# Layer kernel on one Trainium2 core: low parts and sums of squares from POOL to DVE in three stages, and nine gated blocks loaded early

## The chip, the core and the metric

The kernel runs on one core of a Trainium2 chip. The metric is the device time of one execution in microseconds (us), as the median of several runs. A separate profiled execution of the same kernel gives the trace. The engines are PE (TensorE matmul; PEld is its weight load), DVE (VectorE), ACT (ScalarE), POOL (GpSimd) and SP (SyncE), whose queue issues the transfers.

## The reference, cut to what matters

One layer acts on two groups of tokens: 256 prompt tokens and 1024 latent tokens, both of width 1024, with the same weights. The hidden width of the two feed-forward nets (ffn1 and ffn2) is 2816.

```python
def rms_norm(x, g):
    y = xf * lax.rsqrt(jnp.mean(xf * xf, axis=-1, keepdims=True) + EPS)
    return (y * g.astype(jnp.float32)).astype(x.dtype)

def swiglu(h, w_in, w_out):
    gate, up = jnp.split(h @ w_in, 2, axis=-1)
    return (jax.nn.silu(gate) * up) @ w_out

def layer(x, cond, p, lb, lam_init, ctx_cache=None, rope=None):
    ...
    h = rms_norm(x, p['norm_ffn1']) * (1.0 + sc1) + sh1
    x = x + 0.5 * g1 * swiglu(h, p['w_ffn1_in'], p['w_ffn1_out'])
    h = rms_norm(x, p['norm_mix']) * (1.0 + sc2) + sh2
    mix, k_ctx, v_ctx, s_ctx = token_mix(h, p, lb, lam_init, ctx_cache, rope)
    x = x + g2 * mix
    h = rms_norm(x, p['norm_ffn2']) * (1.0 + sc3) + sh3
    x = x + 0.5 * g3 * swiglu(h, p['w_ffn2_in'], p['w_ffn2_out'])
    return x, k_ctx, v_ctx, s_ctx
```

The token mixing between the two nets is not touched by the change, save for the sums of squares of its norm.

## The kernel before, in words

**Arithmetic.** A float32 product is made from split operands. ACT rounds a block to its high part (a CAST), another engine subtracts this from the block and gets the low part (a TENSOR_TENSOR, TT), and PE multiplies high by high, high by low and low by high. So each block of weights or of activations costs one cast, one subtraction and three matmuls for each output tile.

**Stages.** Each net has four: prompt in, latents in, latents out, prompt out. In the trace, ffn1's run at 34.6 to 190.5 us, to about 650, to 885.4 and to 961.5; mixing with attention lies between; ffn2's run at 1936.2 to 2072.4, to about 2499, to 2732.2 and to the end.

- Prompt in (`wload`, L99): 44 units of weights, 128x1024, named `ffn1g0` to `ffn1g21` (gate) and `ffn1u0` to `ffn1u21` (up); a trailing `r` is the raw load, `h` the high and `l` the low part. `wh` and `wl` have four buffers each, so the parts of a unit are made a few units ahead of PE. In this stage (`half` set) DVE and POOL take the low parts in turn. In ffn1, DVE also forms the sums of latents (`o0a`, `o0b`, `x0b` and the like) for the stage that follows.
- Latents out (`latents_out`, `out_blocks`): seven products of a Strassen-like scheme in the order 1, 2, 5, 6, 7, 3, 4, each over eleven blocks p. For each block PE does 12 matmuls of 128x512 with the weight block `ffn1w_{p}b` and the block of gated values `ffn1w_{p}g`. Names carry p and not the product, so each name comes seven times. ACT casts both; POOL makes the low part of b, DVE that of g (L758). For products 5, 6, 7 and 3 DVE also forms the sum that is the block b (`ffn1s`, `ffn1qhh`, `ffn1qhl`), and drains the finished products from PSUM into the latents (`xr0a` and others: SCALAR_TENSOR_TENSOR, STT). With the block tiles in four buffers, the parts are made up to three blocks ahead.
- Gated values go by way of `g_d` in device memory: the last steps of latents in write `g_d` from `ffn1g10c` to `ffn1g10x` and `ffn1t`. Five blocks of product 1 are loaded into a resident tile (`self.g1`, in the trace `ffn1qhl<-g_d`); every later one goes through the four-buffer tag `gr` (`ffn1w_5gr<-g_d`), asked for two blocks ahead.
- Prompt out (`prompt_out_blocks`): 22 steps, each with two weight blocks `ffn1pw` (128x512; the first low part on DVE, the second on POOL) and one block of values `ffn1pvv` (128x256, on DVE), for 24 matmuls of 128x256.
- Sums of squares (`sumsq`, L345): ACT squares (`sq`), and POOL (first half) or DVE (second half) adds to `sacc`, as the drained latents come out; a norm follows (its `pm` matmul waits for `sacc`).

**Order.** A scheduler sets the order of the instructions on each engine from the order of the code and the tiles that come free; once built, each engine works through its list strictly in order. SP issues its loads and stores in order too, and a transfer that waits for its tile or for its data holds those behind it. All instructions are recorded under L49, where a helper class passes them on, so they are told apart by the names of their tiles.

Of the kernel before, what the change touches and what calls it, by code (L numbers as in the profile page):

```python
# [9 lines left out]
F32 = mybir.dt.float32  # L10
# [3 lines left out]
ALU = mybir.AluOpType  # L14
# [4 lines left out]
P = 128  # L19
# [46 lines left out]
class Kern:  # L66
# [9 lines left out]
    def pool(self, name, space=None, side=None):  # L76
        kw = {} if space is None else {"space": space}
        if space != DRAM:
            kw["reuse_waits"] = "tile"
        if side is not None:  # L80
            kw["side"] = side
        return self.tc.tile_pool(name=name, bufs=1, **kw)
# [16 lines left out]
    def wload(self):  # L99
        nc = self.nc  # L100
        if not self.rawq:
            self.rload()
        raw, name = self.rawq.popleft()
        shape = list(raw.shape)
        hi = self.wp.tile(shape, F32R, tag="wh", bufs=4, name=name + "h")
        nc.scalar.copy(hi, raw)
        lo = self.wp.tile(shape, F32R, tag="wl", bufs=4, name=name + "l")
        self.nw += 1
        eng = nc.vector if self.half and self.nw % 2 else nc.gpsimd
        eng.tensor_tensor(lo, raw, hi.bitcast(F32), op=ALU.subtract)  # L110
        self.wready.append((hi, lo))
        while len(self.rawq) < self.nraw and self.wq:
            self.rload()
# [231 lines left out]
    def sumsq(self, tp, c, d):  # L345
        nc = self.nc
        n = CH[c][1]
        h = d // 4
        acc = self.acc[c]
        if h not in acc:  # L350
            acc[h] = tp.tile([P, n], F32, tag="t", bufs=self.tb, name=f"sacc{c}_{h}")
            nc.scalar.activation(acc[h], self.x[c][d], AF.Square)
        else:
            sq = tp.tile([P, n], F32, tag="t", bufs=self.tb, name=f"sq{c}_{d}")
            nc.scalar.activation(sq, self.x[c][d], AF.Square)
            (nc.vector if h else nc.gpsimd).tensor_tensor(acc[h], acc[h], sq, op=ALU.add)
        self.nsq[c] += 1
        if self.nsq[c] == KD:
            self.nsq[c] = 0
            return True  # L360
# [308 lines left out]

    def out_resident(self, hp, wout, name):  # L670

        t = [hp.tile([P, m, 512], F32, tag=g, name=f"{name}q{g}")
             for m, g in ((8, "hh0"), (8, "hl0"), (4, "hh2"), (2, "hl2"), (8, "hl1"))]
        fl = [x[:, j] for x, m in zip(t, (8, 8, 4, 2)) for j in range(m)]
        self.a11, self.a12 = fl[:NPR], fl[NPR:]
        self.s3, self.g1 = [t[4][:, j] for j in range(3)], [t[4][:, j] for j in range(3, 8)]
        for p in range(8):
            self.out_w(wout, self.a11[p], p, 0, 0)
            if p < 5:
                self.nc.sync.dma_start(self.g1[p], self.g_d[:, 0, p])  # L680

    def out_w(self, wout, t, p, i, j):
        self.nc.sync.dma_start(t, wout[0, (2 * p + j) * P:(2 * p + j + 1) * P, i * 512:(i + 1) * 512])
# [11 lines left out]
    def out_blocks(self, wout, name, hp, xp, pool):  # L695

        nc = self.nc
        V, G = nc.vector, nc.gpsimd
        keys = [(i, p) for i in self.OUT for p in range(NPR)]
        raws = {}  # L700
        xs = deque(self.x_pieces(xp))

        def load(j):
            if j >= len(keys):
                return
            i, p = keys[j]
            n_ = f"{name}w{i}_{p}"
            if j < 5:
                g = self.g1[j]
            else:  # L710
                g = pool().tile([P, 512], F32, tag="gr", bufs=4, name=n_ + "gr")
                nc.sync.dma_start(g, self.g_d[:, i - 1, p])
            a = None
            if i == 1:
                if p >= 8:
                    self.out_w(wout, self.a11[p], p, 0, 0)
            elif i == 2:
                self.out_w(wout, self.a12[p], p, 0, 1)
            elif i in (5, 7, 4):
                a = self.raw(pool, [P, 2, 512], n_ + "r")  # L720
                if i in (5, 7):
                    self.out_w(wout, a[:, 0], p, 1, 0)
                if i in (5, 4):
                    self.out_w(wout, a[:, 1], p, 1, 1)
            if xs and j >= 2 and j % 2 == 0:
                nc.sync.dma_start(*xs.popleft())
            if i == 5 and p == 4:
                self.x_move(pool(), 2, True)
            raws[j] = g, a
        s_ = None  # L730
        load(0)
        load(1)
        for j, (i, p) in enumerate(keys):
            load(j + 2)
            g, a = raws.pop(j)
            n_ = f"{name}w{i}_{p}"
            if i == 5 and p == 0:
                s_ = hp.tile([P, 8, 512], F32, tag="hh1", name=f"{name}s")
                s_ = [s_[:, q] for q in range(8)] + self.s3
            if i == 1:  # L740
                a = self.a11[p]
            elif i == 2:
                a = self.a12[p]
            elif i == 5:
                V.tensor_tensor(s_[p], a[:, 0], a[:, 1], op=ALU.add)
                a = s_[p]
            elif i == 6:
                V.tensor_tensor(s_[p], s_[p], self.a11[p], op=ALU.subtract)
                a = s_[p]
            elif i == 7:  # L750
                V.tensor_tensor(self.a11[p], self.a11[p], a[:, 0], op=ALU.subtract)
                a = self.a11[p]
            elif i == 3:
                V.tensor_tensor(self.a12[p], self.a12[p], s_[p], op=ALU.subtract)
                a = self.a12[p]
            else:
                a = a[:, 1]
            yield self.block(a, n_ + "b", G), self.block(g, n_ + "g", V)  # L758

    def latents_out(self, name, pop, g, ng, done, then):  # L760
        nc = self.nc
# [36 lines left out]
    def prompt_out_blocks(self, wout, name, pool):  # L798
        nc = self.nc
        raws = {}  # L800

        def load(f):
            if f < NF:
                r = self.raw(pool, [P, D], f"{name}pw{f}")
                nc.sync.dma_start(r, wout[0, f * P:(f + 1) * P, :])
                v = pool().tile([P, NP], F32, tag="gr", bufs=4, name=f"{name}pv{f}")
                nc.sync.dma_start(v, self.gp_d[:, f])
                raws[f] = r, v
        load(0)
        load(1)  # L810
        for f in range(NF):
            load(f + 2)
            r, v = raws.pop(f)
            w = [self.block(r[:, h * 512:(h + 1) * 512], f"{name}pw{f}{h}", nc.gpsimd if h else nc.vector)
                 for h in range(2)]
            vv = pool().tile([P, 2, NP], F32R, tag="gv", bufs=3, name=f"{name}pvv{f}")
            self.split(vv[:, 0], vv[:, 1], v)
            yield w, vv
# [957 lines left out]
```

## Time and profile before

| | |
|---|---|
| median of 3 runs | 2801.65 us (2801.49 to 2803.29) |
| profiled execution | 2805.98 us |
| its span in the trace | 2803.9 us |
| mean granted PE clock | 0.983 |
| DMA | 429.29 MB, mean 153 GB/s |

The profiled execution is 2.08 us longer than its span and 4.33 us longer than the median. In the views below, a row of the timeline reads: start, duration, engine, line, operation, tile written <- tiles read, shapes, count, and in brackets the idle time before with what ended it. Durations overlap where an engine is pipelined, so the pitch of back-to-back instructions is less than the duration of one. A row of the waits gives the engine and its tile, what it waited for, the total in us, the number of times and the longest.

### The profile page before, as it was taken

How to read it: one execution, taken by the hardware profiler on the slowest of the kernel's cores; microseconds unless marked ns; L12 is line 12 of the kernel's file. 1: busy time of each engine (PE TensorE's matmuls, PEld its weight loads, DVE VectorE, ACT ScalarE, POOL GpSimd, SP SyncE). 2: the span in 40 equal slices, each digit the busy share in tenths (PEclk: the TensorE clock that was granted, in tenths of full speed). 3: DMA queues.
4: the chain of work that ended last, by engine and by line, in shares of the span. 5: the costliest groups of instructions: out<-in, count | busy, mean ns of one | idle time of the engine just before them, and what ended most of it. 6: DMA issues, size and time to landing. Idle time of an engine off the chain costs nothing.

```text
span 2803.9 us, 43921 instructions
## 1 busy us (share of the span) xinstructions
PE 2685.2 (96%) x17070; PEld 2344.7 (84%) x17070; DVE 1675.1 (60%) x2158; ACT 1116.9 (40%) x1896; POOL 1274.7 (45%) x902
## 2 busy tenths in 40 slices
PE   7999999999899999999999899999999999999999
PEld 6887777887688889898989888888988888877789
DVE  3955554655877636465555488747745555558754
ACT  4642222323345423232323477745432333324344
POOL 2454444443545636455554122165454444435443
PEclk8999999999999999999999999999999999999999
DMA  9765656338635531323224944385643233357455
GB/s 304 232 185 184 194 181 196 103 98 271 199 119 191 189 103 55 102 71 96 76 68 124 213 104 115 132 276 160 189 137 113 94 97 110 104 192 249 132 180 185
DMA packets 412245, 429.29 MB, mean 153 GB/s; under 512 B 20621, under 2 KB 314757, under 8 KB 409989
## 3 DMA queue, kind: packets, MB, share of 16 engines
q1 hardware_dynamic: 411856, 426.43, 49.1%
q8 instruction: 134, 2.20, 0.3%
q14 instruction: 75, 0.61, 0.1%
q10 hardware_dynamic: 180, 0.06, 0.0%
HBM read 326.79 MB, written 99.61 MB: 152 GB/s over the span
## 4 chain that ended last, share of the span: by engine, by line
PE 76%; DVE 10%; DMA 4%; issue 4%; POOL 3%; ACT 2%; SPq 1%; ACTq 0%; DVEq 0%; POOLq 0%
PE ffn2po L49 6%; PE ffn1po L49 5%; PE mob L49 4%; PE ffn2pp L49 2%; PE ffn2pu L49 2%; PE ffn2pg L49 2%; PE ffn1pu L49 1%; PE ak0b L49 1%; PE aq0b L49 1%; PE ak1b L49 1%; PE ffn1pg L49 1%; SPq L49 1%; PE ffn1pp L49 1%; PE ada L49 1%; PE hg1b L49 1%
## 5 line engine op out<-in xcount | busy, mean ns | idle before, releaser
L49 PE MATMUL ffn1pp<-ffn1pvv,ffn1pw 128*128 128x256 f32 x528 | 67.9, 290 | 3.7 <-DVE ffn1pvv L49 3.3
L49 PEld LDWEIGHTS ffn1pp<-ffn1pvv,ffn1pw 128*128 128x128 f32 x528 | 66.2, 197 | 5.2 <-DVE ffn1pvv L49 4.1
L49 PE MATMUL ffn2pp<-ffn2pvv,ffn2pw 128*128 128x256 f32 x528 | 64.0, 283 | 0.0
L49 PEld LDWEIGHTS ffn2pp<-ffn2pvv,ffn2pw 128*128 128x128 f32 x528 | 63.6, 192 | 0.1
L49 POOL TENSOR_TENSOR ffn2pw<-ffn2pw,ffn2pw 128x512 fp32r<-128x512 f32 x22 | 28.9, 1316 | 35.8 <-ACT ffn2pw L49 34.2
L49 POOL TENSOR_TENSOR hl<-nt,hh 128x256 fp32r<-128x256 f32 (+1 forms) x20 | 22.4, 1121 | 40.1 <-ACT hh L49 37.7
L49 POOL TENSOR_TENSOR ffn1pw<-ffn1pw,ffn1pw 128x512 fp32r<-128x512 f32 x22 | 33.2, 1512 | 13.2 <-ACT ffn1pw L49 13.1
L49 ACT ACTIVATE nt<-nt,mt,sv 128x256 f32<-128x256 f32 (+1 forms) x40 | 25.7, 680 | 29.9 <-DVE sv L49 17.7
L49 DVE TENSOR_TENSOR sacc<-sacc,sq 128x512 f32<-128x512 f32 (+1 forms) x18 | 29.3, 1630 | 12.3 <-ACT sq L49 12.0
L49 ACT CAST ffn2pw<-ffn2pw 128x512 fp32r<-128x512 f32 x44 | 26.9, 620 | 15.5 <-PE ffn2pp L49 8.8
L49 DVE TENSOR_TENSOR ffn2pw<-ffn2pw,ffn2pw 128x512 fp32r<-128x512 f32 x22 | 17.0, 772 | 25.8 <-ACT ffn2pw L49 25.8
L49 ACT CAST ffn1pw<-ffn1pw 128x512 fp32r<-128x512 f32 x44 | 26.1, 615 | 12.6 <-DMA ffn1pw<-w_ffn_out 6.4
L49 PE MATMUL ada<-wada,cst 128*32 128x256 f32 x448 | 30.0, 385 | 0.0
L49 PE MATMUL ffn1po<-ffn1w_5g,ffn1w_5b 128*128 128x512 f32 x84 | 22.8, 422 | 6.0 <-ACT ffn1w_5g L49 5.3
L49 DVE TENSOR_REDUCE a_0mx<-a_0S 128x1 f32<-128x1536 f32 x8 | 14.1, 1758 | 24.0 <-PE a_0S L49 23.9
L49 PE MATMUL ffn2po<-ffn2w_5g,ffn2w_5b 128*128 128x512 f32 x84 | 22.9, 426 | 5.5 <-ACT ffn2w_5g L49 5.5
L49 PE MATMUL ffn1po<-ffn1w_4g,ffn1w_4b 128*128 128x512 f32 x84 | 22.6, 420 | 4.4 <-POOL ffn1w_4b L49 4.4
L49 PEld LDWEIGHTS ffn1po<-ffn1w_5g,ffn1w_5b 128*128 128x128 f32 x84 | 17.2, 207 | 10.8 <-ACT ffn1w_5g L49 5.7
L49 PE MATMUL ffn2po<-ffn2w_7g,ffn2w_7b 128*128 128x512 f32 x84 | 22.8, 423 | 2.7 <-DVE ffn2w_7g L49 2.7
L49 PEld LDWEIGHTS ffn2po<-ffn2w_5g,ffn2w_5b 128*128 128x128 f32 x84 | 17.2, 208 | 9.6 <-ACT ffn2w_5g L49 5.9
L49 POOL TENSOR_TENSOR sacc<-sacc,sq 128x512 f32<-128x512 f32 (+1 forms) x18 | 24.9, 1386 | 0.5
L49 DVE TENSOR_TENSOR ffn1pw<-ffn1pw,ffn1pw 128x512 fp32r<-128x512 f32 x22 | 19.7, 899 | 8.0 <-ACT ffn1pw L49 8.0
(4066 smaller groups left out, 10302.9 us busy)
## 6 DMA issues: line engine op xcount, KB each, us to landing
wada<-w_ada SPq DMA_DIRECT2D x112, 256.0 KB, 4.4
ffn1r<-w_ffn_in SPq DMA_DIRECT2D x44, 512.0 KB, 4.1
ffn2r<-w_ffn_in SPq DMA_DIRECT2D x44, 512.0 KB, 4.1
ffn1pw<-w_ffn_out SPq DMA_DIRECT2D x22, 512.0 KB, 3.4
ffn2pw<-w_ffn_out SPq DMA_DIRECT2D x22, 512.0 KB, 4.2
g_d<-ffn1t SPq DMA_DIRECT2D x33, 256.0 KB, 2.1
g_d<-ffn2t SPq DMA_DIRECT2D x33, 256.0 KB, 3.0
wadb<-w_ada SPq DMA_DIRECT2D x12, 512.0 KB, 8.8
```

Of the source, the lines that this page charges most:

```text
L49: r = f(*a, **k)
```

## The change

In the three stages named in the title's list (prompt in, latents out, prompt out) of both nets:

- `wload`: in prompt in DVE makes all low parts while `half` is set; of the 44 that POOL made in the two nets together, 42 move and two stay.
- `out_blocks`: DVE makes the low parts of b as well, 77 for each net.
- `prompt_out_blocks`: DVE makes both low parts of `ffn1pw`, 22 more for each net.
- `sumsq`: DVE adds all squares, wherever it is called, 18 adds more.
- `out_resident`: nine gated blocks of product 1 are loaded into resident tiles instead of five. The four new ones (`ffn1ghh`) take the tile `hh2`, in which four weight blocks of product 2 lay; those are given their place when (2, 5) is loaded.

The sum is 42 + 154 + 44 + 18 = 258 TTs that leave POOL for DVE. PE's list of instructions is the same except for two or three places where neighbours swap; ACT's and SP's counts do not change.

```diff
--- before.py
+++ after.py
@@ -106,7 +106,7 @@
         nc.scalar.copy(hi, raw)
         lo = self.wp.tile(shape, F32R, tag="wl", bufs=4, name=name + "l")
         self.nw += 1
-        eng = nc.vector if self.half and self.nw % 2 else nc.gpsimd
+        eng = nc.vector if self.half else nc.gpsimd
         eng.tensor_tensor(lo, raw, hi.bitcast(F32), op=ALU.subtract)
         self.wready.append((hi, lo))
         while len(self.rawq) < self.nraw and self.wq:
@@ -353,7 +353,7 @@
         else:
             sq = tp.tile([P, n], F32, tag="t", bufs=self.tb, name=f"sq{c}_{d}")
             nc.scalar.activation(sq, self.x[c][d], AF.Square)
-            (nc.vector if h else nc.gpsimd).tensor_tensor(acc[h], acc[h], sq, op=ALU.add)
+            nc.vector.tensor_tensor(acc[h], acc[h], sq, op=ALU.add)
         self.nsq[c] += 1
         if self.nsq[c] == KD:
             self.nsq[c] = 0
@@ -669,15 +669,23 @@
 
     def out_resident(self, hp, wout, name):
 
-        t = [hp.tile([P, m, 512], F32, tag=g, name=f"{name}q{g}")
-             for m, g in ((8, "hh0"), (8, "hl0"), (4, "hh2"), (2, "hl2"), (8, "hl1"))]
-        fl = [x[:, j] for x, m in zip(t, (8, 8, 4, 2)) for j in range(m)]
+        def tile_(m, g, n="q"):
+            return hp.tile([P, m, 512], F32, tag=g, name=f"{name}{n}{g}")
+        t = [tile_(8, "hh0"), tile_(8, "hl0"), None, None, tile_(8, "hl1")]
+        fl = [x[:, j] for x in t[:2] for j in range(8)]
         self.a11, self.a12 = fl[:NPR], fl[NPR:]
-        self.s3, self.g1 = [t[4][:, j] for j in range(3)], [t[4][:, j] for j in range(3, 8)]
+        g = tile_(4, "hh2", "g")
+        self.g1 = [t[4][:, j] for j in range(3, 8)] + [g[:, j] for j in range(4)]
+
+        def rest():
+            t = tile_(4, "hh2"), tile_(2, "hl2")
+            self.a12 += [x[:, j] for x, m in zip(t, (4, 2)) for j in range(m)]
+        self.rest12 = rest
+        self.s3 = [t[4][:, j] for j in range(3)]
         for p in range(8):
             self.out_w(wout, self.a11[p], p, 0, 0)
-            if p < 5:
-                self.nc.sync.dma_start(self.g1[p], self.g_d[:, 0, p])
+            self.nc.sync.dma_start(self.g1[p], self.g_d[:, 0, p])
+        self.nc.sync.dma_start(self.g1[8], self.g_d[:, 0, 8])
 
     def out_w(self, wout, t, p, i, j):
         self.nc.sync.dma_start(t, wout[0, (2 * p + j) * P:(2 * p + j + 1) * P, i * 512:(i + 1) * 512])
@@ -705,7 +713,9 @@
                 return
             i, p = keys[j]
             n_ = f"{name}w{i}_{p}"
-            if j < 5:
+            if i == 2 and p == 5:
+                self.rest12()
+            if j < 9:
                 g = self.g1[j]
             else:
                 g = pool().tile([P, 512], F32, tag="gr", bufs=4, name=n_ + "gr")
@@ -755,7 +765,7 @@
                 a = self.a12[p]
             else:
                 a = a[:, 1]
-            yield self.block(a, n_ + "b", G), self.block(g, n_ + "g", V)
+            yield self.block(a, n_ + "b", V), self.block(g, n_ + "g", V)
 
     def latents_out(self, name, pop, g, ng, done, then):
         nc = self.nc
@@ -811,7 +821,7 @@
         for f in range(NF):
             load(f + 2)
             r, v = raws.pop(f)
-            w = [self.block(r[:, h * 512:(h + 1) * 512], f"{name}pw{f}{h}", nc.gpsimd if h else nc.vector)
+            w = [self.block(r[:, h * 512:(h + 1) * 512], f"{name}pw{f}{h}", nc.vector)
                  for h in range(2)]
             vv = pool().tile([P, 2, NP], F32R, tag="gv", bufs=3, name=f"{name}pvv{f}")
             self.split(vv[:, 0], vv[:, 1], v)
```

In the lists below a row is the operation, written <- read, shape, and a count where it repeats at once; `_5828` and the like are numbers of buffers. First, SP's queue at the end of ffn1's latents in, before:

```order
L49 DMA ffn1qhl_5828<-w_ffn_out 128x512 x2
L49 DMA g_d<-ffn1t_5879 128x512
L49 DMA g_d<-ffn1t_5880 128x512
L49 DMA g_d<-ffn1t_5881 128x512
L49 DMA g_d<-ffn1g10x 128x512
L49 DMA xr1a<-xd_75 128x1024
L49 DMA ffn1qhl_5828<-w_ffn_out 128x512
L49 DMA ffn1w_5gr<-g_d 128x512
L49 DMA ffn1w_6gr<-g_d 128x512
L49 DMA ffn1w_7gr<-g_d 128x512
L49 DMA ffn1w_8gr<-g_d 128x512
```

and of the same place in the changed kernel:

```order
L49 DMA g_d<-ffn1g10c 128x512
L49 DMA ffn1qhl_5829<-g_d 128x512 x5
L49 DMA ffn1ghh_5830<-g_d 128x512 x4
L49 DMA xr0a<-xd_74 128x1024
L49 DMA xr0b<-xd_74 128x1024
L49 DMA g_d<-ffn1g10z 128x512
L49 DMA g_d<-ffn1g10y 128x512
L49 DMA ffn1qhl_5828<-w_ffn_out 128x512
```

The loads of blocks 5 to 8 stood behind all writes of `g_d`, one `xr1a` load and the weight loads `ffn1qhl<-w_ffn_out`; as `ffn1ghh` they now stand right behind the five other resident ones, ahead of the `g_d` writes from `ffn1g10z` on.

Second, DVE's list in product 5 of ffn1's latents out, from block 3 to block 5, before:

```order
L49 TENSOR_TENSOR ffn1w_3g<-ffn1w_3gr,ffn1w_3g 128x512
L49 TENSOR_TENSOR ffn1qhl_5831<-ffn1w_9r 128x512
L49 TENSOR_TENSOR ffn1qhl_5831<-ffn1w_10r 128x512
L49 TENSOR_TENSOR ffn1s<-ffn1s,ffn1qhh_5827 128x512
L49 TENSOR_TENSOR ffn1w_4g<-ffn1w_4gr,ffn1w_4g 128x512
L49 TENSOR_TENSOR ffn1s<-ffn1s,ffn1qhh_5827 128x512 x2
L49 TENSOR_TENSOR ffn1qhh_5827<-ffn1qhh_5827,ffn1w_0r 128x512
L49 TENSOR_TENSOR ffn1qhl_5828<-ffn1qhl_5828,ffn1s 128x512
L49 TENSOR_TENSOR ffn1w_5g<-ffn1w_5gr,ffn1w_5g 128x512
```

and in the changed kernel:

```order
L49 TENSOR_TENSOR ffn1w_3b<-ffn1s,ffn1w_3b 128x512
L49 TENSOR_TENSOR ffn1w_3g<-ffn1w_3gr,ffn1w_3g 128x512
L49 SCALAR_TENSOR_TENSOR xr0a<-ffn1po_3_6140,mt_129,xr0a 128x512
L49 TENSOR_TENSOR sacc_0_6464<-sacc_0_6464,sq_1_6490 128x512
L49 TENSOR_TENSOR ffn1w_4b<-ffn1s,ffn1w_4b 128x512
L49 TENSOR_TENSOR ffn1w_4g<-ffn1w_4gr,ffn1w_4g 128x512
L49 TENSOR_TENSOR sacc_0_6464<-sacc_0_6464,sq_2_6517 128x512
L49 TENSOR_TENSOR ffn1s<-ffn1w_7r 128x512
L49 TENSOR_TENSOR ffn1w_5b<-ffn1s,ffn1w_5b 128x512
L49 TENSOR_TENSOR ffn1w_5g<-ffn1w_5gr,ffn1w_5g 128x512
```

The low part of b stands next to that of g, adds of squares (`sacc`) lie between the blocks, and of the sums for later blocks (`ffn1s`, `ffn1qhl`, `ffn1qhh`) only one stands here where there were seven.

Third, DVE's list in ffn1's prompt in, units 10 and 11, before:

```order
L49 TENSOR_TENSOR ffn1g10l<-ffn1g10r,ffn1g10h 128x1024
L49 TENSOR_TENSOR x0b<-o0b_1423,x0b 128x512
L49 TENSOR_TENSOR o0a_1497<-x1a,x0a 128x512
L49 TENSOR_TENSOR o0t_1416<-o0a_1419,o0t_1416 128x512
L49 TENSOR_TENSOR o0t2hl_1418<-o0b_1423,o0t2hh_1417 128x512
L49 TENSOR_TENSOR o0b_1501<-x1b,o0a_1497 128x512
L49 TENSOR_TENSOR ffn1g11l<-ffn1g11r,ffn1g11h 128x1024
L49 TENSOR_TENSOR ffn1s_1255<-ffn1s_1255,ffn1pu_1270 128x256
```

and in the changed kernel:

```order
L49 TENSOR_TENSOR ffn1g10l<-ffn1g10r,ffn1g10h 128x1024
L49 TENSOR_TENSOR o0b_1340<-x0b,o0b_1340 128x512
L49 TENSOR_TENSOR o0a_1419<-x1a,x0a 128x512
L49 TENSOR_TENSOR ffn1u10l<-ffn1u10r,ffn1u10h 128x1024
L49 TENSOR_TENSOR ffn1g11l<-ffn1g11r,ffn1g11h 128x1024
L49 TENSOR_TENSOR o0t_1416<-o0a_1419,o0t_1416 128x512
L49 TENSOR_TENSOR ffn1s_1255<-ffn1s_1255,ffn1pu_1270 128x256
L49 TENSOR_TENSOR o0b_1423<-x1b,o0a_1419 128x512
L49 TENSOR_TENSOR ffn1u11l<-ffn1u11r,ffn1u11h 128x1024
```

Both low parts of a unit (`ffn1g11l`, `ffn1u11l`) now stand in DVE's list among the same operand sums, and the low part of the next unit's gate has come nearer to that of the unit before.

## The prediction, as put on record before the run

> **What bounds the kernel now.** I read the page's totals and its chain first, then the span cut into stages, then PE's waits by what ended them, and last the timeline where those waits lie.
>
> ```profile
> PE 2685.2 (96%) x17070; PEld 2344.7 (84%) x17070; DVE 1675.1 (60%) x2158; ACT 1116.9 (40%) x1896; POOL 1274.7 (45%) x902
> PE 76%; DVE 10%; DMA 4%; issue 4%; POOL 3%; ACT 2%; SPq 1%; ACTq 0%; DVEq 0%; POOLq 0%
> ```
>
> PE is the bound: 96% busy and 76% of the chain. The change takes no matmul away, so it can gain only PE's idle time and the time at a lower granted clock. Those are in the stages (columns: window, length, busy time of PE, PEld, DVE, ACT, POOL, then granted clock, DMA share, GB/s):
>
> ```profile
> 34.60:190.50 155.90, 143.39 (x1125) 139.88 (x1125) 105.50 (x126) 92.06 (x155) 68.11 (x28) 0.95 0.76 226
> 642.60:885.40 242.80, 227.23 (x979) 184.09 (x978) 175.11 (x201) 98.95 (x175) 119.27 (x85) 0.97 0.61 199
> 885.40:961.50 76.10, 70.68 (x547) 68.95 (x546) 63.99 (x83) 46.41 (x86) 49.02 (x31) 0.96 0.56 186
> 1936.20:2072.40 136.20, 130.47 (x1075) 128.68 (x1074) 81.19 (x93) 67.50 (x95) 58.06 (x24) 1.00 0.62 182
> 2491.50:2732.20 240.70, 229.85 (x1008) 188.11 (x1008) 170.79 (x200) 94.33 (x167) 112.61 (x78) 0.97 0.61 201
> 2732.20:2803.90 71.70, 67.20 (x562) 66.92 (x560) 30.25 (x53) 31.60 (x61) 25.31 (x20) 1.00 0.55 183
> ```
>
> The stages that the change touches leave PE idle for 12.5, 15.6, 5.4, 5.7, 10.9 and 4.5 us, 54.6 together, of which the last contains the kernel's end. Where the clock reads 0.95 to 0.97 some busy time is lost too. PE's longest waits in them:
>
> ```profile
> PE ffn2po L49 <- ACT ffn2w_5g L49: 5.5, 1, 5.5
> PE ffn1po L49 <- ACT ffn1w_5g L49: 5.3, 1, 5.3
> PE ffn1pu L49 <- POOL ffn1u11l L49: 4.7, 1, 4.7
> PE ffn1po L49 <- POOL ffn1w_4b L49: 4.4, 1, 4.4
> PE pm L49 <- POOL sacc L49: 2.8, 1, 2.8
> ```
>
> Each is something that the change moves: a late load (`w_5g`), a low part on POOL (`u11l`, `w_4b`), sums of squares.
>
> **The early loads.** The timeline around block 5 of product 1 in ffn1, and the same block in ffn2:
>
> ```profile
> 644.98 0.39 PE L49 MATMUL ffn1u10p<-o0t2hh,ffn1w101s 128*128 128x512 f32 x1
> 658.81 2.88 PE L49 MATMUL ffn1po<-ffn1w_3g,ffn1w_3b 128*128 128x512 f32 x12
> 661.53 2.88 PE L49 MATMUL ffn1po<-ffn1w_4g,ffn1w_4b 128*128 128x512 f32 x12
> 663.34 0.43 SPq L49 DMA_DIRECT2D ffn1w_5gr<-g_d  x1
> 669.00 0.62 ACT L49 CAST ffn1w_5g<-ffn1w_5gr 128x512 fp32r<-128x512 f32 x1 [6.61 <-DMA ffn1w_5gr<-g_d]
> 669.67 4.96 PE L49 MATMUL ffn1po<-ffn1w_5g,ffn1w_5b 128*128 128x512 f32 x12 [5.26 <-ACT ffn1w_5g L49]
> 674.47 2.88 PE L49 MATMUL ffn1po<-ffn1w_6g,ffn1w_6b 128*128 128x512 f32 x12
> ...
> 2510.36 2.88 PE L49 MATMUL ffn2po<-ffn2w_4g,ffn2w_4b 128*128 128x512 f32 x12
> 2518.76 5.39 PE L49 MATMUL ffn2po<-ffn2w_5g,ffn2w_5b 128*128 128x512 f32 x12 [5.53 <-ACT ffn2w_5g L49]
> 2523.99 2.90 PE L49 MATMUL ffn2po<-ffn2w_6g,ffn2w_6b 128*128 128x512 f32 x12
> ```
>
> A clean block has a pitch of 661.53 - 658.81 = 2.72 us. Block 6 starts 12.94 us after block 4 instead of 5.44: 7.5 us lost, 5.4 in the wait and 2.1 in the slower matmuls behind it. In ffn2 it is 13.63 instead of 5.44, 8.2 us. The load was issued at 663.34, two microseconds before its block was due, because SP's queue has the late `g_d` writes ahead of it; it took 5.7 us to the cast. Its new tile `hh2` was last read at 644.98 by `ffn1u10p`, so the new loads can go at about 645.4. Four issues at 0.43 us end at 647, and with the same 5.7 us the last lands near 653; block 5 is due at 664.25. Behind them in SP's queue `xr0a` and the `g_d` writes move back by four issues, 1.7 us, and the weight blocks of product 2 that lose `hh2` come later. The next late load would be `w_9gr`: block 9 is due at 661.53 + 5 x 2.72 = 675.1, and issued no later than `w_5gr` was before it lands at 669. So I take both stalls as gone: **7.5 + 8.2**, lower bound half of it, if block 9 or product 2 is late in its place.
>
> **Low parts and squares in latents out.** The worst stretch of ffn1 lies from block 3 of product 5 to block 2 of product 6, the start of it and its end shown here, and of ffn2 in product 6 and the start of 7:
>
> ```profile
> 723.12 2.06 DVE L49 SCALAR_TENSOR_TENSOR xr0a<-ffn1po,mt,xr0a 128x512 f32<-128x512 f32 x3
> 725.12 7.50 POOL L49 TENSOR_TENSOR sacc<-sacc,sq 128x512 f32<-128x512 f32 x3
> 726.15 2.88 PE L49 MATMUL ffn1po<-ffn1w_3g,ffn1w_3b 128*128 128x512 f32 x12
> 733.86 1.74 DVE L49 TENSOR_TENSOR ffn1s<-ffn1s,ffn1qhh 128x512 f32<-128x512 f32 x1 [5.08 <-POOL ffn1w_4b L49]
> 768.60 2.88 PE L49 MATMUL ffn1po<-ffn1w_2g,ffn1w_2b 128*128 128x512 f32 x12
> ...
> 2567.53 2.88 PE L49 MATMUL ffn2po<-ffn2w_0g,ffn2w_0b 128*128 128x512 f32 x12
> 2614.59 1.75 PE L49 MATMUL ffn2po<-ffn2w_2g,ffn2w_2b 128*128 128x512 f32 x7
> ```
>
> The ten blocks from 726.15 to 768.60 take 42.45 us against 27.2: 15.2 lost. The 13 of ffn2 take 47.06 against 35.4, with about 1.6 us of other PE work between them: 10.1 lost. POOL begins three adds at 725.12 and ends them 7.5 us later; `w_4b` comes behind them on POOL, and DVE, which had waited 5.08 us, goes on at 733.86 when it is done. Beside a busy POOL a DVE operation of this shape takes 1.74 us. How long it takes without one:
>
> ```profile
> 74.98 2.48 DVE L49 TENSOR_TENSOR x0a<-x0a,rb 128x512 f32<-128x512 f32 x4
> 678.14 1.29 POOL L49 TENSOR_TENSOR ffn1w_10b<-ffn1qhl,ffn1w_10b 128x512 fp32r<-128x512 f32 x1 [1.43 <-ACT ffn1w_10b L49]
> 678.62 1.36 DVE L49 TENSOR_TENSOR ffn1w_10g<-ffn1w_10gr,ffn1w_10g 128x512 fp32r<-128x512 f32 x1 [1.36 <-ACT ffn1w_10g L49]
> ```
>
> Four in 2.48 us are a pitch of 0.60, one alone 0.68; three STTs in 2.06 are a pitch of about 0.66. So a low part costs DVE 0.60 us where it cost POOL 1.29, and DVE loses nothing more to POOL: the low part of g, begun at 678.62 while POOL worked, took 1.36 us, twice its own time, which pays for that of b. By the changed list DVE has, from the first b of product 5 to that of 6, 45 TTs and 4 STTs, 45 x 0.60 + 4 x 0.66 = 29.6 us; in the next stretch 41 and 8, 29.9. PE needs 11 x 2.72 = 29.9 for each. In ffn2 it is 48 and 4, 31.4, with PE at 29.9 and its 1.6 of other work, and then 37 and 8, 27.5. DVE comes out level with PE, with three blocks of look-ahead (8 us) to absorb its waits. Level isn't free: I leave 3 us in ffn1 and 2 in ffn2 for casts that DVE waits for in order, so **12 and 8** are saved, lower bound nothing.
>
> **Prompt in.** The waits here are for low parts. In ffn1 DVE is full of sums for the next stage:
>
> ```profile
> 108.71 1.22 DVE L49 TENSOR_TENSOR ffn1g10l<-ffn1g10r,ffn1g10h 128x1024 fp32r<-128x1024 f32 x1
> 109.81 2.40 POOL L49 TENSOR_TENSOR ffn1u10l<-ffn1u10r,ffn1u10h 128x1024 fp32r<-128x1024 f32 x1 [3.30 <-ACT ffn1u10h L49]
> 116.85 7.34 POOL L49 TENSOR_TENSOR ffn1u11l<-ffn1u11r,ffn1u11h 128x1024 fp32r<-128x1024 f32 x1 [4.64 <-ACT ffn1u11h L49]
> 119.00:124.00 5.00, 0.50 (x5) 0.29 (x3) 5.00 (x7) 2.12 (x4) 5.00 (x1) 1.00 0.21 65
> 124.00:129.00 5.00, 4.76 (x27) 4.76 (x28) 5.00 (x5) 2.25 (x4) 2.99 (x2) 0.66 0.77 211
> ```
>
> POOL takes 2.40 us for a unit's part and 7.34 when DVE runs back to back, while PE stands (0.50 busy of 5); the next slice has a clock of 0.66. DVE needs 1.22 for it, about 1.14 in a run. By my count of the changed list, the 16 busiest units cost DVE 44.5 us, against 46.6 of PE (24 matmuls each, at 130.47 / 1075 = 0.121 us in ffn2's stage, where the clock was 1.00). So DVE just holds, and I take **7** of the 12.5 us, from 0 to 10. In ffn2 DVE has no such run for long: **4.5** of 5.7.
>
> At 119 to 124 DVE is busy for the whole slice. The Trainium skill ("Perfetto Trace Analysis", section Optimizing Scalar/DVE Operations) says that with a saturated DVE it may make sense to offload to ScalarE or even to GPSIMD, though the shared SBUF port may spoil that; the change goes against the first half. The 1.36 and 1.74 us beside POOL are rows for the second half. By the first half alone the sum would be that of the second rival below.
>
> **The rest.** The pm wait of 2.8 us at the start of mixing is for three adds on POOL behind other work; DVE adds them at 0.36 each (128x256): **2**. In prompt out two groups show the prices:
>
> ```profile
> L49 POOL TENSOR_TENSOR ffn1pw<-ffn1pw,ffn1pw 128x512 fp32r<-128x512 f32 x22 | 33.2, 1512 | 13.2 <-ACT ffn1pw L49 13.1
> L49 DVE TENSOR_TENSOR ffn1pw<-ffn1pw,ffn1pw 128x512 fp32r<-128x512 f32 x22 | 19.7, 899 | 8.0 <-ACT ffn1pw L49 8.0
> ```
>
> In ffn1's, DVE is already busy for 64.0 of 76.1 us, with the norms of the latents, and gets 22 x 0.60 = 13.2 more, but POOL keeps some of these norms' low parts and so still slows it: 64.0 + 13.2 exceeds 76.1, less what the port gives back. I take **1**, from -4 to 6. In ffn2's, DVE has 30 of 72 us and PE waits for nothing: 0.
>
> Sum: 7.5 + 8.2 + 12 + 8 + 7 + 4.5 + 2 + 1 = 50.2 us. The profiled execution would go from 2805.98 to 2755.8, span 2753.7; the median is 4.33 less than that execution, so 2801.65 - 50.2 = 2751.4, say **2751**. That is 1.8%.
>
> **The rivals.**
>
> *Only the waits on POOL and on loads go, DVE doesn't keep up* (0.22). If runs on DVE are broken by waits, an operation costs its lone 0.68 us: 49 of them 33.3 against 29.9, 3.4 us lost in each of two stretches per net. Then latents out saves 12 - 6 = 6 and 8 - 6 = 2, prompt in of ffn1 2 (16 units at 50 us), prompt out -3; with 15.7, 4.5 and 2 it is 29 us: 2772. For it: the 64 of 76 us in prompt out. Against: the runs at 0.60 in rows with POOL silent.
>
> *DVE becomes the bound outright, slower than before* (0.04). The row of 899 ns is what a DVE low part took on average, beside POOL. If it takes that without POOL too, a stretch of 49 costs 44 us against 29.9; 14.2 us x 4 stretches is 57 against 25 lost now, and prompt in at 1.5 times 44.5 us loses 20 against 9 now; less the 22 us of loads, pm and ffn2's prompt in, the kernel is 21 us slower: 2823. It decides from about 0.82 us an operation. Against it stands that the excess over 0.60 comes with POOL beside it, which goes. This is the case in which the skill's first half would be right.
>
> *Only the early loads count* (0.07): squares and low parts on DVE give back what POOL's gave, so 15.7 and the 2 of pm are left: 2784.
>
> *The loads' stall moves* to block 9 or to product 2 (0.07): 8 us of the sum stay: 2759.
>
> **How the numbers follow.** The forecast has 0.60. Its own range, from the terms' ends that may well fall together (prompt in 0 to 10, latents out 12 to 25, prompt out -4 to 6), is 2739 to 2765. To hold 8 in 10 the range must reach to the first rival and, above the forecast, to more gain than I counted, as all idle time of these stages is 54.6 us and the clock's part comes on top: 2736 to 2774. Two measurements of this kernel can be told apart from about 0.2%, 5.6 us. Only the second rival is slower: 0.04; within 0.2% needs a gain of under 5.6, between that rival and the third: 0.03; faster 0.93.
>
> **What would show it.** Right: blocks 4, 5 and 6 of product 1 at a pitch of 2.72 in both nets, the casts of 5g before 660; products 5 and 6 of ffn1 at 30 to 32 us each, DVE operations in runs of 0.60 and no wait for POOL in these stages; prompt in of ffn1 near 149 us with clock 1.0. Wrong: PE waits for DVE's b and g low parts in a row through products 5 and 6 (first rival), or a new wait for 9g or for a block of product 2. If ffn1's prompt out grows, its term has the wrong sign. If the time is above 2790, DVE's price was wrong throughout.

## The result, and the profile after

The changed kernel takes 2739.79 us (median of 6 runs, 2738.21 to 2741.87), the kernel before 2802.51 in the runs beside it: the medians differ by 62.7 us or 2.2%. The measured ratio is 0.9769 with a 95% interval of 0.9756 to 0.9781, a distance from 1 that is 65 us of 2803. The span of the profiled execution goes from 2803.9 to 2736.4 us, 67.5 less. The forecast was 50 us less. Of all executions behind this document one, of the kernel with the low parts of b alone, took 5324.86 us, for no reason that the record shows, and the ratios leave it out.

The page of the changed kernel, its busy times first and then the chain:

```profile
PE 2658.0 (97%) x17070; PEld 2330.0 (85%) x17070; DVE 1716.5 (63%) x2416; ACT 1118.4 (41%) x1896; POOL 861.5 (31%) x644
PE 58%; DVE 5%; POOL 2%; DMA 1%; issue 1%; ACT 0%; SPq 0%; POOLq 0%; DVEq 0%; ACTq 0%
```

POOL lost 258 instructions and 413 us of busy time. DVE took them over and is busy only 41 us more, 0.16 us for each of them, though one costs it 0.60 us or more: the rest it got back by no longer sharing with POOL.

The stages of the changed kernel (window, length, busy time of PE, PEld, DVE, ACT, POOL, clock, DMA share, GB/s), for prompt in, latents out and prompt out of ffn1, then prompt in and latents out of ffn2:

```profile
34.90:175.10 140.20, 138.18 (x1125) 136.47 (x1126) 104.96 (x144) 92.56 (x154) 10.22 (x7) 0.98 0.84 251
635.10:847.20 212.10, 212.10 (x943) 175.63 (x942) 172.85 (x279) 95.99 (x170) 1.01 (x1) 1.00 0.65 214
847.20:922.20 75.00, 67.37 (x546) 65.65 (x545) 62.58 (x102) 46.43 (x87) 20.67 (x12) 1.00 0.56 191
1894.50:2022.50 128.00, 128.00 (x1076) 127.52 (x1075) 86.94 (x114) 68.41 (x95) 3.57 (x3) 1.00 0.65 193
2450.10:2664.90 214.80, 214.80 (x973) 178.45 (x972) 168.96 (x271) 91.47 (x162) 0.00 (x0) 1.00 0.65 211
```

In three of them PE is busy for the whole stage at a clock of 1.00. In ffn1's latents out it also works at its clean pitch: 77 blocks at 2.72 us are 209.4 of the 212.1 us. ffn1's prompt in has 2.0 us of idle time left, and ffn1's prompt out 7.6 of 75 us. Cut at the first matmul of each stage in both traces (the last row ends at the last matmul of the stage), the lengths are:

| stage | before | after | saved | term of the prediction |
|---|---|---|---|---|
| ffn1 prompt in | 155.9 | 140.2 | 15.7 | 7 |
| ffn1 latents in | 460.1 | 460.0 | 0.1 | - |
| ffn1 latents out | 234.9 | 212.1 | 22.8 | 7.5 + 12 |
| ffn1 prompt out and all up to ffn2 | 1050.8 | 1047.3 | 3.5 | 1 + 2 |
| ffn2 prompt in | 136.2 | 128.0 | 8.2 | 4.5 |
| ffn2 latents in | 426.9 | 427.6 | -0.7 | - |
| ffn2 latents out | 232.9 | 214.8 | 18.1 | 8.2 + 8 |
| ffn2 prompt out | 65.0 | 65.0 | 0 | 0 |

PE's longest waits in the changed kernel: of the five shown before, none is left, and what comes first is in the mixing and in ffn1's prompt out (`ffn1pp`).

```profile
PE h3s L49 <- DVE h3B L49: 6.1, 3, 2.7
PE a_0S L49 <- DMA va_d<-av: 5.3, 1, 5.3
PE ffn1pp L49 <- DVE ffn1pvv L49: 5.3, 4, 2.0
```

The resident loads and the blocks around number 5 of product 1, in the timeline:

```profile
629.39 0.39 PE L49 MATMUL ffn1u10p<-o0t2hh,ffn1w101s 128*128 128x512 f32 x1
629.81 2.02 SPq L49 DMA_DIRECT2D ffn1ghh<-g_d  x4
641.22 0.61 ACT L49 CAST ffn1w_5g<-ffn1ghh 128x512 fp32r<-128x512 f32 x1
645.94 2.88 PE L49 MATMUL ffn1po<-ffn1w_4g,ffn1w_4b 128*128 128x512 f32 x12
646.95 0.49 SPq L49 DMA_DIRECT2D ffn1w_9gr<-g_d  x1
648.66 2.88 PE L49 MATMUL ffn1po<-ffn1w_5g,ffn1w_5b 128*128 128x512 f32 x12
651.38 2.88 PE L49 MATMUL ffn1po<-ffn1w_6g,ffn1w_6b 128*128 128x512 f32 x12
```

The four loads are issued 0.4 us after the last reader of `hh2` begins, block 5 is cast 7.4 us ahead of its matmuls, and the pitch is 2.72. DVE a few us ahead of the passage to another product (the last row is shown for its wait):

```profile
712.15 0.68 DVE L49 TENSOR_TENSOR ffn1w_9b<-ffn1qhl,ffn1w_9b 128x512 fp32r<-128x512 f32 x1
712.76 0.68 DVE L49 TENSOR_TENSOR ffn1w_9g<-ffn1w_9gr,ffn1w_9g 128x512 fp32r<-128x512 f32 x1
713.36 1.28 DVE L49 TENSOR_TENSOR ffn1qhl<-ffn1qhl,ffn1qhl 128x512 f32<-128x512 f32 x2
714.56 0.68 DVE L49 TENSOR_TENSOR ffn1qhh<-ffn1qhh,ffn1w_0r 128x512 f32<-128x512 f32 x1
715.17 0.68 DVE L49 TENSOR_TENSOR ffn1w_10b<-ffn1qhl,ffn1w_10b 128x512 fp32r<-128x512 f32 x1
715.77 0.68 DVE L49 TENSOR_TENSOR ffn1w_10g<-ffn1w_10gr,ffn1w_10g 128x512 fp32r<-128x512 f32 x1
...
723.50 0.69 DVE L49 TENSOR_TENSOR ffn1qhh<-ffn1qhh,ffn1w_5r 128x512 f32<-128x512 f32 x1 [1.02 <-DMA ffn1w_5r<-w_ffn_out]
```

Each row starts 0.60 us after the one before (two operations take 1.20), which is the pitch that before had with POOL silent, and both low parts of a block are among them. Between 705 and 745 DVE stops only twice, 1.02 us for the load in the last row and 0.69 for another.

### The profile page after: what moved, and what is told of

Same layout as the page of the kernel before. It is cut to its first block, busy times and chain, and to the rows that moved or that the text cites. A ratio compares the mean times of both kernels' runs of the same rounds, so it can differ in the third digit from the quotient of the medians.

```text
span 2736.4 us, 43768 instructions
## 1 busy us (share of the span) xinstructions
PE 2658.0 (97%) x17070; PEld 2330.0 (85%) x17070; DVE 1716.5 (63%) x2416; ACT 1118.4 (41%) x1896; POOL 861.5 (31%) x644
## 4 chain that ended last, share of the span: by engine, by line
PE 58%; DVE 5%; POOL 2%; DMA 1%; issue 1%; ACT 0%; SPq 0%; POOLq 0%; DVEq 0%; ACTq 0%
PE ffn2po L49 8%; PE mob L49 4%; PE ffn2pp L49 2%; PE ffn2pg L49 2%; PE ffn2pu L49 2%; PE ffn1pp L49 1%; PE hi0b L49 1%; PE aq0b L49 1%; PE ak0b L49 1%; PE ak1b L49 1%; PE av1b L49 1%; PE hg1b L49 1%; PE hg0b L49 1%; PE hi1b L49 1%; PE ffn2u10p L49 1%
## 5 line engine op out<-in xcount | busy, mean ns | idle before, releaser
L49 POOL TENSOR_TENSOR nr<-nm,nh 128x4 f32<-128x4 f32 (+1 forms) x9 | 9.0, 1005 | 275.8 <-DVE nm L49 275.8
L49 DVE TENSOR_TENSOR sacc<-sacc,sq 128x512 f32<-128x512 f32 (+1 forms) x36 | 44.7, 1251 | 12.8 <-ACT sq L49 12.5
L49 DVE TENSOR_TENSOR ffn1pw<-ffn1pw,ffn1pw 128x512 fp32r<-128x512 f32 x44 | 34.5, 813 | 7.9 <-ACT ffn1pw L49 7.9
L49 DVE TENSOR_TENSOR ffn2pw<-ffn2pw,ffn2pw 128x512 fp32r<-128x512 f32 x44 | 30.0, 690 | 13.7 <-ACT ffn2pw L49 12.1
L49 PEld LDWEIGHTS ada<-wada,cst 128*32 128x32 f32 x448 | 11.7, 109 | 14.7 <-issue 9.9
L49 PE MATMUL ffn1po<-ffn1w_10g,ffn1w_10b 128*128 128x512 f32 x84 | 20.6, 394 | 0.0
L49 PE MATMUL ffn2po<-ffn2w_4g,ffn2w_4b 128*128 128x512 f32 x84 | 20.4, 391 | 0.0
L49 PE MATMUL ffn1po<-ffn1w_8g,ffn1w_8b 128*128 128x512 f32 x84 | 20.3, 391 | 0.0
L49 PE MATMUL ffn2po<-ffn2w_6g,ffn2w_6b 128*128 128x512 f32 x84 | 20.3, 390 | 0.0
```

The lines of the kernel that those rows point to most:

```text
L49: r = f(*a, **k)
```

## The experiments

Each kernel is compared with the kernel before on the same chip. A figure such as "13.5 us less" is the ratio's distance from 1 times 2803 us; the stage lengths are from the profiled execution of each, cut as in the table above. One execution is one sample: ffn1's prompt in takes 155.9, 153.2, 153.6 and 156.8 us in the kernel before and the first three below, which share its code there, so a difference of 3 us in one stage says little. Theory: the gain is in independent parts (the loads; low parts in latents out; low parts in prompt in), and it is there because DVE makes a low part in 0.60 us once POOL is silent.

**The loads alone.** The kernel before with these hunks only:

```diff
+        g = tile_(4, "hh2", "g")
+        self.g1 = [t[4][:, j] for j in range(3, 8)] + [g[:, j] for j in range(4)]
...
-            if j < 5:
+            if i == 2 and p == 5:
+                self.rest12()
+            if j < 9:
```

> Before, with the nine resident blocks alone; all low parts and squares stay where they were. If the stalls at block 5 of product 1 are a matter of the load's place in SP's queue, they go whole: 7.5 + 8.2 = 15.7 us less than before, about 2787 (2784 to 2790), and blocks 4, 5, 6 have a pitch of 2.72. Rival, the stall moves on to block 9 or to a weight block of product 2: 5 us or less, 2797 or more.

Measured: 0.9952 (0.9940 to 0.9963), 13.5 us less. Latents out goes from 234.9 to 227.0 us in ffn1 and from 232.9 to 225.3 in ffn2, 15.5 together. PE's waits in ffn1's latents out, where 5.3 us for the cast of `5g` led the list before:

```profile
PE ffn1po L49 <- POOL ffn1w_4b L49: 3.9, 1, 3.9
PE pm L49 <- DVE sacc L49: 1.7, 1, 1.7
```

The stall didn't move on to block 9 or to product 2; the wait for POOL's low part stayed.

**The low parts of b alone.** The kernel before with

```diff
-            yield self.block(a, n_ + "b", G), self.block(g, n_ + "g", V)
+            yield self.block(a, n_ + "b", V), self.block(g, n_ + "g", V)
```

> Before, with the low parts of b in latents out on DVE alone; squares half on POOL, loads late. If the low parts on POOL (1.29 us each, and DVE slowed beside them) make the losses in products 5 and 6, then 18 to 25 us less than before, about 2781, with the wait at 5g kept. Rival, the squares on POOL make them (three adds took 7.5 us ahead of one low part): under 8 us less, 2794 or more.

Measured: 0.9907 (0.9878 to 0.9936), 26 us less; latents out 219.3 and 222.3 us, 26.2 less together. The largest wait left in ffn1's is the one for the load:

```profile
PE ffn1po L49 <- ACT ffn1w_5g L49: 4.6, 1, 4.6
```

**The adds of squares alone.** The kernel before with

```diff
-            (nc.vector if h else nc.gpsimd).tensor_tensor(acc[h], acc[h], sq, op=ALU.add)
+            nc.vector.tensor_tensor(acc[h], acc[h], sq, op=ALU.add)
```

> Before, with all adds of squares on DVE alone. If the low parts of b are the main cause, then what goes is the one wait of 4.4 us with the slow matmuls behind it in each net and the pm wait: 5 to 11 us less than before, about 2794. Rival, the squares are the main cause: 20 us or more less, 2782 or less.

Measured: 1.0004 (0.9990 to 1.0017), no change, which neither expected. In ffn1's latents out PE's wait for `w_4b` got shorter, from 4.4 to 2.4 us, but did not go (the last row is POOL's, of the same place):

```profile
PE ffn1po L49 <- ACT ffn1w_5g L49: 5.0, 1, 5.0
PE ffn1po L49 <- POOL ffn1w_4b L49: 2.4, 1, 2.4
PE pm L49 <- DVE sacc L49: 1.7, 1, 1.7
...
728.79 5.85 POOL L49 TENSOR_TENSOR ffn1w_4b<-ffn1s,ffn1w_4b 128x512 fp32r<-128x512 f32 x1 [1.31 <-ACT ffn1w_4b L49]
```

That stage got 2.7 us shorter and the next, prompt out, 3.2 longer. So the squares were not the main cause of the losses in products 5 and 6, though they stood right before the longest wait. With them gone from POOL, its low part `w_4b` is itself recorded for 5.85 us, while DVE runs back to back beside it. ffn2 had the same before the change, with no add ahead:

```profile
2577.98 7.89 POOL L49 TENSOR_TENSOR ffn2w_6b<-ffn2s,ffn2w_6b 128x512 fp32r<-128x512 f32 x1 [2.53 <-ACT ffn2w_6b L49]
```

**The low parts of prompt in alone.** The kernel before with

```diff
-        eng = nc.vector if self.half and self.nw % 2 else nc.gpsimd
+        eng = nc.vector if self.half else nc.gpsimd
```

> Before, with the low parts of prompt in on DVE alone. If the two stages' gain after the change (15.7 and 8.2 us) is the low parts' own, about 24 us less than before, 2778. Rival, part of it came with the squares on DVE or from what was earlier in the program: 15 us or less, 2787 or more.

Measured: 0.9919 (0.9896 to 0.9943), 23 us less. Its two stages take 142.6 and 128.0 us, 13.3 and 8.2 less. Latents out, which this edit leaves alone, came out 1.3 and 3.9 us shorter too. With the loads' 13.5 and the 26 of latents out the sum of the parts is 62, against 62.7 (medians) to 65 (ratio) for all of the change: the parts add up, as far as intervals of 3 to 8 us each can tell.

**All but the loads.** The changed kernel with the five resident blocks of before (the first experiment's hunks taken back):

> The changed kernel with five resident blocks as before. If the loads' gain adds to the rest, the stalls at block 5 are back: 15.7 us more than the changed kernel, about 2755, in waits for the cast of 5g. Rival, with DVE's list less held by POOL the writes of gated values and so the loads come earlier anyway: 3 us more or less.

Measured: 0.9808 (0.9794 to 0.9823), so 0.0039 or 11 us more than the changed kernel's 0.9769. The stages are 6.9 and 5.8 us longer. The wait is back, shorter than before in ffn2 (5.5 us then):

```profile
PE ffn1po L49 <- ACT ffn1w_5g L49: 4.5, 1, 4.5
PE ffn2po L49 <- ACT ffn2w_5g L49: 3.9, 1, 3.9
```

Most of the loads' gain adds to the rest; about 3 of the 15.7 us the rest would have brought anyway, as the profiles go.

**A useless operation on POOL.** The changed kernel with, in `out_blocks`,

```diff
+            b = self.block(a, n_ + "b", V)
+            if j >= 9:
+                x = pool().tile([P, 512], F32, tag="dm", bufs=1, name=n_ + "dm")
+                G.tensor_tensor(x, a, a, op=ALU.mult)
...
```

> The changed kernel with one more operation on POOL for each block of latents out from block 9 of product 1 on (68 for each net): POOL multiplies the block b by itself into a tile that nobody reads. No engine waits for it. If a busy POOL takes time from DVE (0.7 us or more for each overlapping operation), DVE's 29.6 and 29.9 us of work in products 5 and 6 grow past PE's 29.9 by about 8 us each: 20 to 40 us more than the changed kernel, 2760 to 2780, with DVE operations of 1.2 us and over. Rival, POOL's own slowness was the only cost and DVE was merely waiting for its results: within 3 us of the changed kernel.

Measured: 0.9972 (0.9961 to 0.9983), 57 us more than the changed kernel, where the theory of a busy POOL gave 20 to 40. Latents out in ffn1 (first row, the stage) and then POOL and DVE in it:

```profile
636.80:883.30 246.50, 223.38 (x944) 180.29 (x943) 217.44 (x279) 96.12 (x171) 105.08 (x69) 0.97 0.57 184
```

```profile
710.51 10.99 POOL L49 TENSOR_TENSOR ffn1w_7dm<-ffn1s 128x512 f32<-128x512 f32 x1 [8.14 <-DVE ffn1s L49]
721.58 1.55 POOL L49 TENSOR_TENSOR ffn1w_8dm<-ffn1qhl 128x512 f32<-128x512 f32 x1
723.20 1.37 POOL L49 TENSOR_TENSOR ffn1w_9dm<-ffn1qhl 128x512 f32<-128x512 f32 x1
724.65 1.37 POOL L49 TENSOR_TENSOR ffn1w_10dm<-ffn1qhl 128x512 f32<-128x512 f32 x1
...
719.92 0.68 DVE L49 TENSOR_TENSOR ffn1s<-ffn1s,ffn1qhh 128x512 f32<-128x512 f32 x1
721.53 0.69 DVE L49 TENSOR_TENSOR ffn1s<-ffn1s,ffn1qhh 128x512 f32<-128x512 f32 x1 [0.94 <-POOL ffn1w_7dm L49]
722.14 1.53 DVE L49 TENSOR_TENSOR ffn1w_9b<-ffn1qhl,ffn1w_9b 128x512 fp32r<-128x512 f32 x1
723.59 1.52 DVE L49 TENSOR_TENSOR ffn1w_9g<-ffn1w_9gr,ffn1w_9g 128x512 fp32r<-128x512 f32 x1
```

The stage is 34.4 us longer (ffn2's 23.7) with the same 279 instructions on DVE, which are busy for 217 us instead of 173. While DVE runs back to back, the POOL operation is not done: 10.99 us, until DVE stops for once. After that both have work queued, and they go by turns, one DVE operation each 1.45 us where it was 0.60; the turns last until 751 us, for 20 operations of POOL. The stop itself was my experiment's: DVE was to overwrite a block that the useless operation had yet to read, so once in the stage an engine did wait for it, 0.94 us. That wait is not the 34 us; in this place it is what let POOL in.

**A useless operation on DVE.** The same edit with `V` in the place of `G`:

> The changed kernel with one more 128x512 operation of 0.60 us on DVE for each block of latents out from block 9 of product 1 on (68 for each net), whose result nobody reads. If DVE is level with PE in products 5 and 6, as counted, 6.6 us more in each of them and 2 in product 2, less 8 us of look-ahead in each net: 12 to 28 us more than the changed kernel, 2752 to 2768. Rival, DVE had time to spare there: 4 us more or less.

Measured: 0.9824 (0.9809 to 0.9839), 0.0055 or 15 us more than the changed kernel; latents out is 10.1 and 5.7 us longer. So 68 operations on DVE's own list cost a quarter of what 68 on POOL cost, and DVE has no more than the look-ahead to spare there: it is level with PE, as counted. PE's waits in ffn1's latents out are now small and spread over many blocks; three of the longest:

```profile
PE ffn1po L49 <- ACT ffn1w_7b L49: 1.6, 2, 1.3
PE ffn1po L49 <- ACT ffn1w_6b L49: 1.3, 1, 1.3
PE ffn1po L49 <- ACT ffn1w_8b L49: 1.3, 1, 1.3
```

**Prompt out back on POOL.** The changed kernel with

```diff
-            w = [self.block(r[:, h * 512:(h + 1) * 512], f"{name}pw{f}{h}", nc.vector)
+            w = [self.block(r[:, h * 512:(h + 1) * 512], f"{name}pw{f}{h}", nc.gpsimd if h else nc.vector)
```

> The changed kernel with the second low part of the weight blocks of prompt out back on POOL. If this part of the change is worth about 1 us in ffn1 and nothing in ffn2, the time is within 2 us of the changed kernel, 2738 to 2743. Rival, POOL beside a full DVE costs more than the low parts: 5 us more or over; or, the other way, DVE's overload in ffn1 is relieved: 4 us less.

Measured: 0.9789 (0.9772 to 0.9807) against the changed kernel's 0.9769 (0.9756 to 0.9781): 5.6 us more, but the intervals overlap, so the total doesn't settle it. In the profile ffn1's prompt out takes 78.4 us instead of 75.0, ffn2's 65.0 as ever. The other profiles say more about ffn1's: with half of these low parts on POOL it took 75.9 us in the kernel before and 79.1 to 81.0 in the four experiments that added one part of the change; with all on DVE it takes 74.4 to 75.8 in the six profiles that leave the norms as they are. The part has the sign that was forecast and is probably worth more than the 1 us.

**Four on one chip.** The changed kernel again, as the base for the next three:

> The changed kernel itself, as the base for the other three on the same chip: 2740.

Measured: 0.9775 (0.9759 to 0.9792), 2740.99 us.

The changed kernel with half of the adds of squares back on POOL (the third experiment's hunk taken back):

> The changed kernel with half of the adds of squares back on POOL. If the squares matter only while POOL has low parts to make behind them, taking them off POOL is worth nothing by now: within 3 us of the changed kernel. Rival, each add on POOL still holds DVE up while DVE is level with PE in products 5 and 6: 4 us more or over, in latents out.

Measured: 0.9755 (0.9742 to 0.9769), 2735.70 us. Latents out is 212.1 and 214.8 us, as without; so moving the squares to DVE buys nothing that shows here.

The changed kernel with POOL out of the norms:

```diff
-            if d % 2:
-                nc.vector.tensor_copy(hi[:, d], t)
-                nc.vector.tensor_tensor(lo[:, d], t, hi[:, d].bitcast(F32), op=ALU.subtract)
-            else:
-                nc.scalar.copy(hi[:, d], t)
-                nc.gpsimd.tensor_tensor(lo[:, d], t, hi[:, d].bitcast(F32), op=ALU.subtract)
+            nc.scalar.copy(hi[:, d], t)
+            nc.vector.tensor_tensor(lo[:, d], t, hi[:, d].bitcast(F32), op=ALU.subtract)
```

> The changed kernel with POOL out of the norms too: all their low parts on DVE (half were on POOL), all their casts on ACT (half were on DVE). If DVE, slowed by POOL, is what holds PE up in ffn1's prompt out (it was full in 870 to 890 while PE had 15.2 of 20 us), 4 to 8 us less than the changed kernel in that stage. Rival, the chain cast, low part, matmul on ACT becomes as long: no change or slower.

Measured: 0.9755 (0.9742 to 0.9768), 2735.47 us. ffn1's prompt out is 70.2 us, 5.5 less than in the changed kernel on this chip, as the theory had it. As a whole the time is about 5 us less than 2740.99, with intervals that overlap, and other stages of this one execution were longer (prompt in 142.3, latents in 461.7). The stage's row in the changed kernel on this chip, and here:

```profile
847.40:923.10 75.70, 69.90 (x546) 68.61 (x545) 63.77 (x102) 46.79 (x87) 20.93 (x12) 0.95 0.57 190
851.00:921.20 70.20, 66.89 (x546) 65.44 (x545) 57.73 (x102) 50.24 (x95) 9.81 (x4) 1.00 0.62 203
```

The two rows differ in the granted clock as well, 0.95 and 1.00. Against the changed kernel's first profile, which had 1.00 in this stage, the gain is 4.8 us.

And with only the norms' casts on ACT:

```diff
-                nc.vector.tensor_copy(hi[:, d], t)
+                nc.scalar.copy(hi[:, d], t)
```

> The changed kernel with only the norms' casts moved from DVE to ACT; POOL keeps its half of their low parts. DVE loses 8 casts for each latent chunk, 3 us in ffn1's prompt out: 2 to 3 us less than the changed kernel, and less gain than with POOL out. Rival, POOL's part isn't what slows DVE there: as much as with POOL out, or more.

Measured: 0.9762 (0.9749 to 0.9776), 2735.85 us; prompt out 74.4 us, 1.3 less:

```profile
850.10:924.50 74.40, 69.86 (x546) 68.54 (x545) 59.94 (x94) 51.41 (x96) 20.80 (x13) 0.95 0.59 194
```

(The casts are four for each chunk, eight in the stage.) DVE has 94 operations here and is busy for 59.94 us; in the kernel ahead of this one, which put a low part in the place of each cast, it has 102 and is busy for 57.73. So POOL beside it does slow DVE there. How much of the 5.5 us that is stays open, since the clock differed too: PE's idle time in the stage fell by 2.5 us there and by 1.3 us here.

## Why the prediction was right, and where its sizes were off

**Direction and mechanism.** The terms for the loads, for latents out and for prompt in have the sign that was given, each shown by a run of its own; the loads came out at their size and the others above it. DVE's price was the one taken: 0.60 us in runs, in the rows above. DVE kept up where it was counted level with PE: products 5 and 6 of ffn1 take 29.92 us each (first matmuls at 694.90, 724.82 and 754.74), where 30 to 32 were forecast. That a low part on POOL cost as much as it did because the two engines hold each other up, and not by DVE's own load, is shown by the useless operation: put on POOL, with no result that PE needs, it made latents out longer than before the change (246.5 against 234.9 us), and put on DVE it cost a quarter.

**The early loads, 7.5 + 8.2.** Shown: 15.5 us in the stages when done alone. The issue time worked out from the last reader of `hh2` came true to 0.1 us, and neither block 9 nor product 2 came late.

**Latents out, 12 and 8.** Measured 15.6 and 10.6 in the kernel with the low parts alone, against 15.2 and 10.1 lost in the worst stretches. I had left 5 us for DVE's waits in order; DVE's list does have such waits, the 1.02 us for a load of product 7, but the look-ahead took them. The step that failed in part is the cause named ahead of this sum: the three adds of squares that hold `w_4b` for 7.5 us. Moving the adds alone brought nothing that the total shows, and moving them back costs nothing. In the trace of before, 3.7 of the 7.5 us passed in the first add (recorded for 4.81 us) until DVE's run ended at 728.79; after it the three needed about 1.26 us each. Without the adds it was the low part itself that stood beside DVE's run, for the 5.85 us shown above, and in ffn2 for 7.89. DVE's run makes the wait, whichever operation of POOL stands there.

**Prompt in, 7 and 4.5.** The most mis-sized terms: 15.7 (13.3 when done alone) and 8.2. The first is also beyond its upper end of 10, and the stage takes 140.2 us where 149 was forecast. I took a share of the idle time, 12.5 and 5.7 us. PE's busy time fell too: 143.39 to 138.18 us in ffn1 and 130.47 to 128.00 in ffn2, for the same matmuls. In ffn1 that goes with a granted clock of 0.95 that became 0.98. In ffn2 the clock read 1.00 in both, and 2.5 us had been hidden as busy time all the same: a mean of 0.121 us for each of 1075 matmuls against 0.119. In the whole kernel PE's busy time fell by 27.2 us, from 2685.2 to 2658.0, for the same 17070 matmuls. Idle time alone was no upper bound for the gain. The count of DVE's work was right, but my caution (7 of 12.5, for a DVE that "just holds") was not needed. The middle of the stage, before and after:

```profile
104.00:150.00 46.00, 39.03 (x303) 37.85 (x301) 44.69 (x52) 29.45 (x47) 21.39 (x7) 0.96 0.66 191
104.00:150.00 46.00, 46.00 (x386) 46.00 (x384) 44.25 (x65) 29.21 (x44) 0.00 (x0) 1.00 0.83 234
```

DVE is as full as before, but does 65 operations instead of 52, and PE is never idle.

**The rest, 2 and 1.** 3.5 us between the start of ffn1's prompt out and ffn2; a second execution of the changed kernel gave 6.8 there, so the 3 can be neither confirmed nor refuted in size; the kernel with the loads alone, which has neither part, gave 4.5. That the wait of 2.8 us for `sacc` on POOL went is plain in the list of waits; that the squares' move paid for it is not, since it had shrunk to 0.7 us in the kernel with the loads alone too.

**The range.** Its own working has a slip: with latents out at 12 (both nets), ffn1's prompt in at 0 and prompt out at -4 the sum is 30 us and the time 2771, not 2765. The measured 2739.79 us lies at the other end, near 2739: latents out without the loads gave about 25 us, its upper end, and ffn1's prompt in went past its own.

**The rivals.** The rule to offload a saturated DVE ("Perfetto Trace Analysis" of the Trainium skill, section Optimizing Scalar/DVE Operations) has its condition met here in stretches (DVE is busy for 44.69 of the 46 us above), and its second half decides: the useless operation shows that work given to POOL comes back to DVE as waiting. The rival in which DVE doesn't keep up, and the one in which it becomes the bound, did not come about in the changed kernel: PE has no wait for a low part in either latents out. That DVE is close to it is shown by its own useless operation, 15 us. The rival that only the loads count is refuted by the kernels without them, and the one that their stall moves by the kernel with them alone.

What stays open: whether the version without POOL in the norms, or the one with half of the squares on POOL, beats the changed kernel. Each is 5 us less on one chip, at the edge of what the runs can tell. How large the terms of the rest are stays open too.

## What to carry to other kernels

When two engines share the work of small operations on the same data, look up what an operation takes on each while the other is silent and while it runs; if it doubles beside the other, the engine with the lower price alone may do both shares for the price of one. Count the moved work against the bound engine's pitch, stage by stage and from the order's own list, and let that decide, not the share of busy time. And bound a gain by the bound engine's work at full pace, not by its idle time: stretched instructions hide in busy time.

## What the runs showed of the hardware

DVE and POOL behave here as if each operation of this kind (two operands from on-chip memory) held something that both need, to its end. A DVE run without gaps keeps it: a POOL operation of 1.3 us was recorded for 5.85, 7.89 and 10.99 us beside such runs, and ended 0.9 to 1.2 us after DVE had stopped. Once POOL has got in with work queued behind, they take turns, and a DVE operation of 0.60 us comes every 1.45 us. I had expected a loss of about 0.7 us for an overlapping operation; in turns it is 0.85, and it lasts as long as POOL has operations queued, here from 722 to 751 us.
